# Logits of two heads at a time: three split products on all 128 rows in place of fp32 products on 64 rows

## The chip, the cores and the metric

One NeuronCore of one Trainium2 chip runs the kernel; the other cores are idle. The metric is the device time of one execution in microseconds (us). The engines are named as in the profile: PE is TensorE (its weight loads stand as PEld), DVE is VectorE, ACT is ScalarE, POOL is GpSimd and SP is SyncE, which issues most DMAs here.

## The reference, cut to what matters

The network is a diffusion-transformer block of two layers (differential attention, pooling mixer, each with an FFN), followed by a second block with three attention branches over the same 256 tokens of width 1024, all in float32. The change lies in the second block alone. There the logits of every branch are

```python
# branch A: index scores, exact top-k of the keys, 8 query heads on one key head
rel = jax.nn.relu(jnp.einsum("bqhd,bsd->bqhs", iqb, ik))           # 4 index heads
logits = jnp.einsum("bqhd,bqkd->bhqk", qb, kg) * scale + bias
# branch B: 8 query heads on 2 key heads; compressed, selected and window keys
lc = jnp.einsum("bqghd,bngd->bghqn", qb, kcmp) * scale             # 16 compressed keys
ls = jnp.einsum("bqghd,bgqkd->bghqk", qb, kg) * scale + bias_s
lw = jnp.einsum("bqghd,bkgd->bghqk", qb, kwb) * scale + bias_w
# branch C: 12 heads in three dilated groups under one softmax
```

with heads of 64 features. Each is followed by a masked softmax and the weighted sum of the values; the branches' outputs go through projections and gates and are added.

## The kernel before, in words

All tokens stand as two tiles of 128 (`t` = 0, 1). Features that are contracted lie on the partitions, which are the rows of PE. Large products are made of three: operands are split into a high part of type float32r and the rest (`wsplit`, L57: ACT writes `hi`, DVE `lo` = raw - `hi`), and `mm3` (L77) issues hi*hi, hi*lo and lo*hi. These are lines 78 to 80 in every view.

The second block (from L863) first normalises and transposes the residual stream into `hT` (`to_hT`, L300, PE transposes at L308). Then for each branch it runs `project` (L913: h times a slice of `w_in_2`, two PSUM banks), the normalisation of heads (`head_rstd`, L929), the transposition of queries and keys (`normed_T`, L951; `normed_dup_T`, L961, which puts the same key head on both halves of the partitions), the attention (`attend`, L973), `split_oT` (L1011), `gates` (L1020) and `branch` (L1032). A transposed pair of heads fills 128 partitions, one head on each half. `transpose_to` (L940) transposes on PE (L944) and copies from PSUM with one ACT instruction (L949) into `qT` (two buffers) or the key tile `kk` (`ktile`, L876, one buffer), both plain float32. In branch A the index queries and keys are copied by DVE (L1076, L1077).

`attend` makes the logits of four heads (three in branch C) for one token tile: for each head one fp32 matmul with 64 rows, 128 query columns as weights and `nk` = 128 (t = 0) or 256 (t = 1) keys as the moving operand (L987). Heads of different halves write to different banks of the two-bank tag `s`. Then DVE adds the bias and takes the minimum (L989), ACT does the exponential (L996, joint L992), PE transposes the weights (L1002), DVE copies them (L1003) and PE multiplies by the values (L1007). The index scores of branch A (L1087) and the compressed keys of branch B (L1198, 16 keys a head) are also fp32 products on 64 rows.

The order on each engine is a planner's: it goes by program order as priority and by its own costs, and takes later products (gates and the next projections) where the next ones in program order are not ready. Each engine then runs its list strictly in order. POOL's queue at the start of the block is: load `small` (masks, L887), zero `pr2` (L892), load the small parameters into it (L893, L895), load the bias tiles `W` (L910). PE transposes `pr2` (L897), and the key gains that `normed_dup_T` uses come from there. The top-k of branch A is a run of DVE instructions (L1098, L1099).

Of the kernel before, what the change touches and what calls it, by code (L numbers as in the profile page):

```python
# [31 lines left out]
def tile_net(ctx: ExitStack, tc: tile.TileContext, I: dict, out: bass.AP):  # L32
# [24 lines left out]
    def wsplit(raw, a, b, slot=None):  # L57
        """hi and lo parts of a weight unit; the slots rotate over those of wp (0, 1) and the extra pools."""
# [43 lines left out]
    def mod_group(layer, g):  # L102
        """acc [128, 1024]: summed over its partitions it is the g-th sixth of the modulation."""
# [29 lines left out]
    # relative-position bias rows, by distance 255 .. -127, masks included, with their sign changed; 23 copies in DRAM  # L133
# [20 lines left out]
    # the background stream of modulation work: a generator advanced between weight units  # L154
# [69 lines left out]
    def behind(*ins):  # L224
        """on their engines, what follows is issued after ins."""
# [5 lines left out]
    class Norm:  # L231
        """normalisation over the features, with the tokens on the partitions, a tile of 128 of them after the other."""
# [6 lines left out]
        def pre(self, t, n, P, grow):  # L239
            """half n of tile t of ALPHA times the residual stream plus grow * P, and its sum."""  # L240
# [5 lines left out]
        def squares(self, t, n, v, bias):  # L246
            """the part of half n in the mean of (v + 32 * bias) squared."""
# [10 lines left out]
        def normalise(self, t):  # L258
            """tile t less its mean, over its standard deviation."""
# [11 lines left out]
        def layer_norm(self, t, rows):  # L271
            """the residual stream is tile t less its mean, over its standard deviation, times rows[0], plus rows[1]."""
# [12 lines left out]
        def rms(self, t):  # L285
            """z = tile t of the residual stream over its root mean square."""
# [6 lines left out]
        def residual(self, t, rows):  # L293
            """the residual stream is the affine of the normalised tile."""
# [5 lines left out]
        def to_hT(self, t, hT, A, B=None):  # L300
            """tile t of hT = split of z * A + B, transposed."""
# [14 lines left out]
        def pair(self, b, t, k, hh, hl, A, B):  # L316
            """two chunks of to_hT, from k on."""
# [10 lines left out]
    def ln_rows(l, w):  # L328
        """gain and bias of a layer norm on all partitions."""
# [6 lines left out]
    class Out:  # L336
        """output projection mov^T @ w, a PSUM bank for a half of the features of a tile of tokens; rows of w two
        chunks a unit, the last units held back so that the tiles end one after the other."""
# [22 lines left out]
        def finish(self, t, n):  # L361
            """the bank of half n of tile t."""
# [4 lines left out]
    class Ffn:  # L367
        """the FFN's input products, of the first FIRST pairs of hidden chunks tile by tile."""
# [89 lines left out]
    with tc.tile_pool(name="at", bufs=1, side="right", reuse_waits="tile") as at:  # L458
# [43 lines left out]
        def mod_quarter(q):  # L502
            """modc's columns of the chunks 2q and 2q + 1: the scales plus 1 and the shifts of x and ctx."""
# [41 lines left out]
        class Chunk:  # L545
            """256 columns of w_qkv (two heads of q, k or v): loaded once, the products by chunks of k."""
# [44 lines left out]
        with behind(seq["mod"]):  # L591
# [19 lines left out]
            # lambda  # L611
# [40 lines left out]
            # the maps lie on different halves of the PE rows: taking turns, their products overlap  # L652
# [21 lines left out]
        def head_out(aTs, vt, g, sm):  # L674
            """the two heads' outputs of both tiles, normalised and transposed into oT[:, 2g:2g + 2, :]."""
# [51 lines left out]
        # output projection  # L727
# [8 lines left out]
    def norm_loop(nm, P, row, tail, between=None):  # L736
        """pre, normalise and tail of both tiles; what the second starts with fits the waits of the first."""
# [23 lines left out]
    # FFN of layer 0  # L761
    with tc.tile_pool(name="hid", bufs=1, side="right", reuse_waits="tile") as hidp:
# [8 lines left out]
        # the mixing table and what the mixing makes of the shift, alike for all tokens, wait in the place of hT  # L771
# [6 lines left out]
        def mix(dst, t, q, lhs, first):  # L778
            """dst [128, 256] += the tokens of tile t mixed by pm[:, t, q]: their window's mean less the token itself."""
# [94 lines left out]
    with tc.tile_pool(name="b2", bufs=1, reuse_waits="tile") as b2:  # L874
        # the branches take turns with these
        def ktile():  # L876
            return b2.tile([128, 6, 256], F32, tag="kk", name="kk", bufs=1)
# [7 lines left out]
        # small parameters  # L885
# [27 lines left out]
        def project(c0, n, *after):  # L913
            """two PSUM banks: h2 @ w_in[:, c0:c0 + n] for the two token tiles."""
# [14 lines left out]
        def head_rstd(views, nh):  # L929
            """1 / rms of each 64-wide head of the given [128, nh, 64] views, as [128, len(views) * nh]."""  # L930
# [9 lines left out]
        def transpose_to(dst, src, n, scale=None):  # L940
            """dst [128, n, 128] = transposes of the n [128, 128] blocks of src."""
# [3 lines left out]
            bv = b[:, :n * 128].rearrange("p (n c) -> p n c", n=n)  # L945
# [134 lines left out]
        for t in range(2):  # L1080
# [7 lines left out]
            for h2 in range(2):  # L1088
                se.activation(rel[:, h2:4:2, :nk], Sb[h2][:, :, :nk], AF.Relu)
# [280 lines left out]
```

## Time and profile before

| | us |
|---|---|
| three runs | 1171.26, 1172.57, 1173.49 |
| median | 1172.57 |
| profiled execution: span from the first to the last instruction | 1172.5 |
| PE busy, share of the span | 1140.1 (97%) |
| DVE busy | 815.7 (70%) |
| ACT busy | 568.1 (48%) |
| POOL busy | 78.7 (7%) |

The page gives no time of the profiled execution besides its span, so the span stands for its own time; it lies 0.07 us under the median. Busy is the union of an engine's instructions. Consecutive matmuls overlap in the pipeline: a matmul's own duration is longer than the distance from its start to the start of the next, and the distance is what it costs when PE has always something to do. One fp32 matmul of the program stands in the trace as two MATMUL records, a float32r matmul as one.

### The profile page before, as it was taken

The numbers are of one execution on the slowest core, as the hardware profiler recorded it, in microseconds if no ns is written. First come the engines' busy times: TensorE is split into PE (matmuls) and PEld (weight loads), VectorE is DVE, ScalarE is ACT, GpSimd is POOL, SyncE is SP. The second block draws the span as 40 slices with busy tenths as digits, with TensorE's granted clock in tenths as the row PEclk, the third lists the DMA queues.
The fourth block names the chain that finished last, engine by engine and source line by source line (L and its number), as shares of the span: only waits on it lengthen the run. The fifth ranks groups of instructions, "written<-read, shape, count | busy, mean of one in ns | idle before, by whom it ended". The sixth has DMA issues, their size and how long they took to land.

```text
span 1172.5 us, 19786 instructions
## 1 busy us (share of the span) xinstructions
PE 1140.1 (97%) x7973; PEld 1031.5 (88%) x7973; DVE 815.7 (70%) x1511; ACT 568.1 (48%) x994; POOL 78.7 (7%) x151
## 2 busy tenths in 40 slices
PE   5999999999999999999999899999999999999998
PEld 3889988889999877999988688987999898999986
DVE  4787887887887877766644897776676575655542
ACT  4653443475444436644452754444345265544430
POOL 0011100100111111000000101000000000000000
PEclk8999999999999999999999999999999999999999
DMA  9947555648988993866665443740456145655630
GB/s 309 319 146 233 159 165 180 212 148 267 324 306 298 368 340 104 268 211 233 234 215 171 135 163 108 205 159 10 136 163 218 57 161 175 216 180 181 199 125 36
DMA packets 147274, 229.69 MB, mean 196 GB/s; under 512 B 5420, under 2 KB 118715, under 8 KB 147182
## 3 DMA queue, kind: packets, MB, share of 16 engines
q1 hardware_dynamic: 131616, 176.10, 46.0%
q0 software_dynamic: 14672, 50.63, 13.0%
q10 hardware_dynamic: 894, 1.69, 0.4%
q8 instruction: 63, 1.03, 0.4%
q14 instruction: 29, 0.24, 0.1%
HBM read 226.36 MB, written 2.04 MB: 195 GB/s over the span
## 4 chain that ended last, share of the span: by engine, by line
PE 85%; DVE 7%; issue 4%; ACT 3%; DMA 1%; POOL 0%; SPq 0%; ACTq 0%; POOLq 0%; DVEq 0%
PE mm L78 23%; PE mm L80 23%; PE mm L79 23%; PE s L987 3%; PE tp L1007 2%; DVE wlo L71 2%; PE s L658 1%; PE tp L1002 1%; PE tp L682 1%; DMA raw<-in_w_mod_dram 1%; PE s L118 1%; PE s L511 1%; PE s L510 1%; ACT whi L70 1%; PE tp L944 1%
## 5 line engine op out<-in xcount | busy, mean ns | idle before, releaser
L71 DVE TENSOR_TENSOR wlo<-raw,whi 128x1024 fp32r<-128x1024 f32 (+1 forms) x328 | 383.8, 1192 | 155.4 <-ACT whi L70 155.0
L70 ACT CAST whi<-raw 128x1024 fp32r<-128x1024 f32 (+1 forms) x328 | 325.7, 1028 | 236.7 <-PE mm L79 96.7
L80 PE MATMUL mm<-hTh,wlo 128*128 128x256 f32 x1056 | 299.5, 284 | 0.0
L78 PE MATMUL mm<-hTh,whi 128*128 128x256 f32 x1056 | 298.9, 283 | 0.0
L79 PE MATMUL mm<-hTl,whi 128*128 128x256 f32 x1056 | 298.3, 282 | 0.0
L79 PEld LDWEIGHTS mm<-hTl,whi 128*128 128x128 f32 x1056 | 199.1, 189 | 1.4 <-issue 1.3
L78 PEld LDWEIGHTS mm<-hTh,whi 128*128 128x128 f32 x1056 | 199.1, 188 | 1.5 <-issue 0.7
L80 PEld LDWEIGHTS mm<-hTh,wlo 128*128 128x128 f32 x1056 | 199.1, 189 | 0.6 <-issue 0.3
L78 PE MATMUL mm<-whi,hTh 128*128 128x256 f32 (+4 forms) x592 | 186.2, 315 | 2.4 <-DVE hTh L324 2.3
L79 PE MATMUL mm<-wlo,hTh 128*128 128x256 f32 (+4 forms) x592 | 184.6, 312 | 2.0 <-DVE wlo L71 2.0
L80 PE MATMUL mm<-whi,hTl 128*128 128x256 f32 (+4 forms) x592 | 184.8, 313 | 0.4 <-DVE hTl L325 0.4
L78 PEld LDWEIGHTS mm<-whi,hTh 128*128 128x128 f32 x592 | 112.4, 190 | 10.2 <-DVE hTh L324 3.0
L79 PEld LDWEIGHTS mm<-wlo,hTh 128*128 128x128 f32 x592 | 112.3, 190 | 6.5 <-DVE wlo L71 2.7
L80 PEld LDWEIGHTS mm<-whi,hTl 128*128 128x128 f32 x592 | 112.3, 190 | 5.7 <-issue 1.0
L112 DVE SCALAR_TENSOR_TENSOR acc<-mraw,csil,acc 128x1024 f32<-128x1024 f32 x80 | 102.0, 1278 | 8.2 <-DMA mraw<-in_w_mod_dram 7.8
L78 PE MATMUL mm<-whi,hid 128*128 128x512 f32 x264 | 104.2, 395 | 0.0
L79 PE MATMUL mm<-wlo,hid 128*128 128x512 f32 x264 | 104.1, 394 | 0.0
L80 PE MATMUL mm<-whi,hid 128*128 128x512 f32 x264 | 103.7, 393 | 0.0
L111 POOL DMA_DIRECT2D mraw<-in_w_mod_dram x80 | 42.6, 533 | 363.7 <-DVE acc L112 291.4
L79 PEld LDWEIGHTS mm<-wlo,hid 128*128 128x128 f32 x264 | 49.5, 188 | 11.6 <-issue 1.0
L80 PEld LDWEIGHTS mm<-whi,hid 128*128 128x128 f32 x264 | 49.5, 188 | 11.5 <-issue 0.7
L78 PEld LDWEIGHTS mm<-whi,hid 128*128 128x128 f32 x264 | 49.5, 188 | 11.4 <-issue 0.7
(318 smaller groups left out, 1501.7 us busy)
## 6 DMA issues: line engine op xcount, KB each, us to landing
raw<-in_ffn_w_in_dram SPq DMA_DIRECT2D x44, 1024.0 KB, 6.3
mraw<-in_w_mod_dram POOLq DMA_DIRECT2D x80, 512.0 KB, 5.2
raw<-in_ffn_w_out_dram SPq DMA_DIRECT2D x22, 1024.0 KB, 5.5
raw<-in_w_ffn_in_dram SPq DMA_DIRECT2D x22, 1024.0 KB, 5.2
raw<-in_w_in_dram SPq DMA_DIRECT2D x16, 1024.0 KB, 5.2
raw<-in_attn_w_qkv_dram SPq DMA_DIRECT2D x12, 1024.0 KB, 7.5
raw<-in_w_ffn_out_dram SPq DMA_DIRECT2D x11, 1024.0 KB, 5.1
raw<-in_w_in_dram SPq DMA_DIRECT2D x14, 768.0 KB, 4.4
```

The source lines that it names most:

```text
L70: se.copy(hv[:, sl], raw[:, sl])
L71: seq["sub"] = ve.tensor_sub(lv[:, sl], raw[:, sl], hv[:, sl].bitcast(F32)).ins
L78: pe.matmul(o, lh, rh, start=first, stop=False, **kw)
L79: pe.matmul(o, lh, rl, start=False, stop=False, **kw)
L80: return pe.matmul(o, ll, rh, start=False, stop=last, **kw).ins
L111: gp.dma_start(raw, wv[:, k, g * 1024:(g + 1) * 1024])
L112: ve.scalar_tensor_tensor(acc, raw, csil[:, k, 0:1], acc, op0=ALU.mult, op1=ALU.add)
L118: pe.matmul(b[:, j:j + 1], acc[:, j * 128:(j + 1) * 128], ones[:, 0:1], start=True, stop=True)
L510: pe.matmul(o, lh4[:, k, :], wh, start=k == 0 and w == 0, stop=False, **kw)
L511: pe.matmul(o, lh2[:, k, :], wl, start=False, stop=k == 7, **kw)
L987: pe.matmul(So[i], q[hs, pr, tk], kT[hs, :nk], start=True, stop=True)
L1007: pe.matmul(po[:, c:c + 64], pT[:, kt, i, :], heads[i][5](kt), start=kt == 0 and (not joint or i == 0), stop=kt == t and (not joint or i = ...
```

## The change

Operands of the logits are kept in float32r as a high and a low part. Queries: `qT` becomes [128, pair, hi/lo, 256] with one buffer instead of two. Keys: one tile `KZ` [128, 6, hi/lo, half, 256] for all branches takes the place of `kk`. In its slice `half` only the 64 partitions of that half hold keys; the others are zeroed once by POOL at the start of the block. One matmul with all 128 rows of a query pair as weights and both slices as moving operand (2 x `nk` columns) then gives the logits of both heads, and three such products (hi*hi, lo*hi, hi*lo) make the result. The same goes for the index scores and, with a tile `kcZ`, for the compressed keys. Each copy from PSUM is now an ACT instruction for `hi` and a DVE instruction for `lo`, twice for keys (once for each half of the partitions). In branch C the heads are taken in pairs, so two softmaxes are under way at a time; the transposed weights `pT` are three buffers of 128 keys instead of two of 256. The scratch that software DMAs get in SBUF is set to 4096 bytes a partition. Comments are dropped throughout. The core of the diff:

```diff
-        def ktile():
-            return b2.tile([128, 6, 256], F32, tag="kk", name="kk", bufs=1)
+        KZ = b2.tile([128, 6, 2, 2, 256], F32R, name="KZ")
+        for half in range(2):
+            gp.memset(KZ[(1 - half) * 64:(2 - half) * 64, :, :, half, :].bitcast(F32), 0.0)
...
-        def transpose_to(dst, src, n, scale=None):
+        def transposed(src, n):
             b = tbank()
             for i in range(n):
                 pe.transpose(b[:, i * 128:(i + 1) * 128], src[:, i * 128:(i + 1) * 128], ident)
-            bv = b[:, :n * 128].rearrange("p (n c) -> p n c", n=n)
-            if scale is None:
-                se.copy(dst, bv)
-            else:
-                se.activation(dst, bv, AF.Copy, scale=scale)
+            return b[:, :n * 128].rearrange("p (n c) -> p n c", n=n)
+        def put(hi, lo, src, scale):
+            se.activation(hi, src, AF.Copy, scale=scale)
+            ve.scalar_tensor_tensor(lo, src, scale, hi.bitcast(F32), op0=ALU.mult, op1=ALU.subtract)
+        def put_k(src, t, d0, scale=1.0):
+            n, tk = src.shape[1], slice(t * 128, (t + 1) * 128)
+            for half in range(2):
+                p = slice(half * 64, (half + 1) * 64)
+                put(KZ[p, d0:d0 + n, 0, half, tk], KZ[p, d0:d0 + n, 1, half, tk], src[p],
+                    scale if isinstance(scale, float) else scale[p])
+        def put_q(dst, src, t, d0, scale=1.0):
+            n, tk = src.shape[1], slice(t * 128, (t + 1) * 128)
+            put(dst[:, d0:d0 + n, 0, tk], dst[:, d0:d0 + n, 1, tk], src, scale)
...
-                transpose_to(dst[:, d0:d0 + nh, t * 128:(t + 1) * 128], tmp, nh, scale)
+                put_k(transposed(tmp, nh), t, d0, scale)
...
+        def pair_scores(t, q, pr, kz, nk):
+            S = sbank().rearrange("p (a b) -> p a b", a=2)[:, :, :nk]
+            tk = slice(t * 128, (t + 1) * 128)
+            for i, (a, b) in enumerate(((0, 0), (1, 0), (0, 1))):
+                pe.matmul(S, q[:, pr, a, tk], KZ[:, kz, b, :, :nk], start=i == 0, stop=i == 2)
+            return S
...
-            Sb = [sbank().rearrange("p (a b) -> p a b", a=2) for _ in range(2)]
-            So = [(Sb[i // 2][:, i % 2, :nk] if joint else Sb[heads[i][2]][:, i // 2, :nk]) for i in range(n)]
-            for i in range(n):
-                q, pr, hf, kT, W, v = heads[i]
-                hs = slice(hf * 64, (hf + 1) * 64)
-                pe.matmul(So[i], q[hs, pr, tk], kT[hs, :nk], start=True, stop=True)
...
-            pT = b2.tile([128, 2, 4, 128], F32, tag="pT", name="pT", bufs=2)
+            pT = [b2.tile([128, 4, 128], F32, tag="pT", name="pT", bufs=3) for _ in range(t + 1)]
...
+        def attend(t, q, g, kz, W, po, v):
+            nk = 128 * (t + 1)
+            lg, mx = soft_tiles()
+            Ss = [pair_scores(t, q, 2 * g + i, kz, nk) for i in range(2)]
+            for i in range(2):
+                logits(nk, Ss[i], [W(2 * i), W(2 * i + 1)], lg, mx, (2 * i, 2 * i + 1))
+            return weigh(t, 4, lg, mx, False, po, [(64 * i, v) for i in range(4)])
...
-            ve.tensor_copy(iqT[:, :, tk], b[:, 0:256].rearrange("p (n c) -> p n c", n=2))
-            ve.tensor_copy(ikT[:, tk], b[:, 256:384])
-        normed_dup_T(PA, 0, 1, kAT, 0, GA)
+            bv = b[:, 0:384].rearrange("p (n c) -> p n c", n=3)
+            put_q(iqT, bv[:, 0:2], t, 0)
+            put_k(bv[:, 2:3], t, 0)
+        normed_dup_T(PA, 0, 1, 1, GA)
...
-        qT = b2.tile([128, 6, 256], F32, tag="qT", name="qT", bufs=2)
+        qT = b2.tile([128, 6, 2, 256], F32R, tag="qT", name="qT", bufs=1)
...
+        kcZ = b2.tile([128, 2, 2, 2, 16], F32R, name="kcZ")
+        gp.memset(kcZ.bitcast(F32), 0.0)
...
+            Sc = sbank()[:, 0:128].rearrange("p (r h n) -> p r h n", r=4, h=2)
+            for pr in range(4):
+                for i, (a, c) in enumerate(((0, 0), (1, 0), (0, 1))):
+                    pe.matmul(Sc[:, pr], qT[:, pr, a, tk], kcZ[:, pr // 2, c], start=i == 0, stop=i == 2)
...
+            for jp in range(2):
+                soft = [soft_tiles() for _ in range(2)]
+                for g in range(3):
+                    S = pair_scores(t, qT, 2 * g + jp, 2 * g + jp, nk)
+                    for i in range(2):
+                        logits(nk, S[:, i:i + 1], [WC[g][:, 2 * jp + i, 256 - nk:256]], *soft[i], (g,))
...
-    nc = _bacc.Bacc("TRN2", target_bir_lowering=False, num_devices=1)
+    nc = _bacc.Bacc("TRN2", target_bir_lowering=False, num_devices=1, dynamic_dma_scratch_size=4096)
```

## Rows read from the trace of the kernel before

**Rows 1.** The page: span, part 1 (busy share by engine), part 4 (the chain).
```profile
span 1172.5 us, 19786 instructions
PE 1140.1 (97%) x7973; PEld 1031.5 (88%) x7973; DVE 815.7 (70%) x1511; ACT 568.1 (48%) x994; POOL 78.7 (7%) x151
PE 85%; DVE 7%; issue 4%; ACT 3%; DMA 1%; POOL 0%; SPq 0%; ACTq 0%; POOLq 0%; DVEq 0%
```
**Rows 2.** Windows of the second block: stretch, length, busy by engine, clock, DMA.
```profile
core 0: us, PE busy (x) PEld busy (x) DVE busy (x) ACT busy (x) POOL busy (x), PEclk, DMA share, GB/s
676.00:696.00 20.00, 19.59 (x133) 16.84 (x132) 19.70 (x79) 11.38 (x17) 0.00 (x0) 1.00 0.48 161
...
782.00:823.00 41.00, 41.00 (x280) 31.84 (x280) 28.77 (x123) 20.52 (x74) 3.59 (x7) 1.00 0.12 34
...
845.00:902.00 57.00, 55.44 (x330) 54.14 (x328) 40.61 (x92) 28.65 (x43) 0.00 (x0) 1.00 0.60 188
...
sum 291.00, PE 287.76 PEld 259.15 DVE 209.93 ACT 136.69 POOL 12.71; mean PE 31.97 PEld 28.79 DVE 23.33 ACT 15.19 POOL 1.41
```
**Rows 3.** Groups by line on PE, 660 to 955 us: the products on 64 rows.
```profile
L987 PE MATMUL s<-kk,qT 64*128 64x128 f32 (+1 forms) x144 | 32.7, 358 | 0.0
...
L1198 PE MATMUL s<-kcT,qT 64*128 64x16 f32 x32 | 3.2, 262 | 0.0
...
L1087 PE MATMUL s<-kk 64*128 64x128 f32 (+1 forms) x16 | 1.9, 350 | 0.0
```
**Rows 4.** Timeline of PE (start, us): 64-row runs between others, the first and last included.
```profile
675.76 0.71 PE L1087 MATMUL s<-kk 64*128 64x128 f32 x8
...
700.50 0.28 PE L78 MATMUL mm<-hTh,whi 128*128 128x256 f32 x1
700.71 0.48 PE L987 MATMUL s<-kk,qT 64*128 64x128 f32 x2
701.13 0.33 PE L1002 MATMUL tp<-idsel,lg 128*128 128x128 f32 x1
701.39 0.48 PE L987 MATMUL s<-kk,qT 64*128 64x128 f32 x2
...
924.81 0.70 PE L987 MATMUL s<-kk,qT 64*128 64x256 f32 x2
925.44 0.39 PE L79 MATMUL mm<-hTl,whi 128*128 128x256 f32 x1
925.66 0.28 PE L80 MATMUL mm<-hTh,wlo 128*128 128x256 f32 x1
```
**Rows 5.** Timeline of PE: float32r products of 512 columns; of 256 after transposes.
```profile
672.10 0.40 PE L79 MATMUL mm<-wlo,hTh 128*128 128x512 f32 x1
672.34 0.39 PE L80 MATMUL mm<-whi,hTl 128*128 128x512 f32 x1
...
709.25 0.36 PE L80 MATMUL mm<-hTh,wlo 128*128 128x256 f32 x1
709.46 0.28 PE L78 MATMUL mm<-hTh,whi 128*128 128x256 f32 x1
709.58 0.28 PE L79 MATMUL mm<-hTl,whi 128*128 128x256 f32 x1
```
**Rows 6.** Groups by line and shape, DVE and ACT, 660 to 955 us: nearest to the copies.
```profile
L957 DVE TENSOR_TENSOR qn<-mm,rs 128x384 f32<-128x384 f32 x8 | 4.1, 552 | 0.1
...
L1046 DVE SCALAR_TENSOR_TENSOR yacc<-gate,mm 128x512 f32<-128x512 f32 x4 | 2.7, 679 | 1.5 <-PE mm L80 1.5
...
L1076 DVE COPY kk<-tp 128x256 f32<-128x256 f32 x2 | 0.8, 411 | 0.0
L1077 DVE COPY kk<-tp 128x128 f32<-128x128 f32 x2 | 0.6, 276 | 0.0
...
L949 ACT ACTIVATE kk<-tp,pc 128x384 f32<-128x384 f32 x4 | 2.2, 583 | 1.1 <-PE tp L944 1.1
```
**Rows 7.** POOL: its zero fills before 660 us (groups by line), its first load after (timeline).
```profile
L105 POOL MEMSET acc<- 128x1024 f32 x10 | 9.6, 957 | 97.7 <-DVE hcTl L543 51.7 <-PE s L118 20.0 <-ACT f L323 18.9
...
663.63 0.54 POOL L887 DMA_DIRECT2D small<-in_k_small_dram  x1 [78.25 <-ACT z L291]
```

More of the change, by code (lines that the diff above doesn't have):

```diff
@@ L1002, in attend, with soft_tiles @@
                     pe.transpose(b[:, i * 128:(i + 1) * 128], lg[:, i, kt * 128:(kt + 1) * 128], ident)
-                ve.tensor_copy(pT[:, kt, :n, :], b[:, :n * 128].rearrange("p (n c) -> p n c", n=n))
-            for i in range(n):
-                c = po_cols[i]
+                ve.tensor_copy(pT[kt][:, :n, :], b[:, :n * 128].rearrange("p (n c) -> p n c", n=n))
+            for i, (c, v) in enumerate(vs):
                 for kt in range(t + 1):
-                    pe.matmul(po[:, c:c + 64], pT[:, kt, i, :], heads[i][5](kt),
+                    pe.matmul(po[:, c:c + 64], pT[kt][:, i, :], v(kt),
                               start=kt == 0 and (not joint or i == 0), stop=kt == t and (not joint or i == n - 1))
             return mx[:, 12:13] if joint else mx[:, 12:12 + n]
+        def soft_tiles():
+            return (b2.tile([128, 4, 256], F32, tag="lg", name="lg", bufs=2),
+                    b2.tile([128, 16], F32, tag="mx", name="mx", bufs=3))
+        def attend(t, q, g, kz, W, po, v):
[5 more added lines that the diff above has]
+            return weigh(t, 4, lg, mx, False, po, [(64 * i, v) for i in range(4)])
         def split_oT(o_t, nb, oTh, oTl, t):
@@ L1063, in tile_net @@
         iwc = b2.tile([128, 2, 4], F32, name="iwc")
-        kA = ktile()
-        iqT, ikT, kAT = kA[:, 0:2, :], kA[:, 2, :], kA[:, 3:4, :]
+        iqT = b2.tile([128, 2, 2, 256], F32R, tag="vv", name="iqT", bufs=1)
         for t in range(2):
@@ L1083, in tile_net @@
             rel = b2.tile([128, 4, 256], F32, tag="lg", name="rel", bufs=2)
-            Sb = [sbank().rearrange("p (a b) -> p a b", a=2) for _ in range(2)]
-            for h in range(4):
-                hs = slice((h % 2) * 64, (h % 2 + 1) * 64)
-                pe.matmul(Sb[h % 2][:, h // 2, :nk], iqT[hs, h // 2, tk], ikT[hs, :nk], start=True, stop=True)
-            for h2 in range(2):
-                se.activation(rel[:, h2:4:2, :nk], Sb[h2][:, :, :nk], AF.Relu)
+            for pr in range(2):
+                se.activation(rel[:, 2 * pr:2 * pr + 2, :nk], pair_scores(t, iqT, pr, 0, nk), AF.Relu)
             sco = b2.tile([128, 512], F32, tag="so", name="sco", bufs=2)[:, 0:256]
@@ L1116, in tile_net @@
                 po = tbank()
-                den = attend(t, [(qT, 2 * hg + i // 2, i % 2, kAT[:, 0, :], Wm[:, i, :nk], lambda kt: vA[:, kt, :])
-                                 for i in range(4)], False, po, [0, 64, 128, 192])
+                den = attend(t, qT, hg, 1, lambda i: Wm[:, i, :nk], po, lambda kt: vA[:, kt, :])
                 rden = b2.tile([128, 4], F32, tag="rden", name="rden", bufs=2)
@@ L1176, in tile_net @@
         pe.transpose(b[:, 0:32], cks[:, 2:4, :].rearrange("p a c -> p (a c)"), ident[:32, :32])
-        kcT = b2.tile([128, 32], F32, name="kcT")
-        se.activation(kcT, b[:, 0:32], AF.Copy, scale=GB)
+        kcZ = b2.tile([128, 2, 2, 2, 16], F32R, name="kcZ")
+        gp.memset(kcZ.bitcast(F32), 0.0)
+        for half in range(2):
+            p = slice(half * 64, (half + 1) * 64)
+            put(kcZ[p, :, 0, half, :], kcZ[p, :, 1, half, :], b[p, 0:32].rearrange("p (g n) -> p g n", g=2), GB[p])
         b = tbank()
@@ L1183, in tile_net @@
         PQ = project(964, 512)
-        qT = b2.tile([128, 6, 256], F32, tag="qT", name="qT", bufs=2)
-        normed_T(PQ, 0, 8, qT, 0, QS)
+        qT = b2.tile([128, 6, 2, 256], F32R, tag="qT", name="qT", bufs=1)
+        to_q = lambda b, t, d0, q=qT: put_q(q, b, t, d0, QS)
+        normed_T(PQ, 0, 8, 0, to_q)
         WB = [wtile(8), wtile(12)]
@@ L1192, in tile_net @@
             co = b2.tile([128, 5, 8], F32, tag="co", name="co", bufs=2)
-            Sc = [sbank()[:, 0:64].rearrange("p (h n) -> p h n", n=16) for _ in range(2)]
-            for h in range(8):
-                hs = slice((h % 2) * 64, (h % 2 + 1) * 64)
-                g = h // 4
-                pe.matmul(Sc[h % 2][:, h // 2, :], qT[hs, h // 2, tk], kcT[hs, g * 16:(g + 1) * 16], start=True, stop=True)
+            Sc = sbank()[:, 0:128].rearrange("p (r h n) -> p r h n", r=4, h=2)
+            for pr in range(4):
+                for i, (a, c) in enumerate(((0, 0), (1, 0), (0, 1))):
+                    pe.matmul(Sc[:, pr], qT[:, pr, a, tk], kcZ[:, pr // 2, c], start=i == 0, stop=i == 2)
             pcb = b2.tile([128, 8, 16], F32, tag="pc", name="pc", bufs=1)
-            for h2 in range(2):
-                ve.tensor_add(pcb[:, h2:8:2, :], Sc[h2], nmask[:, t, None, 0:16].to_broadcast([128, 4, 16]))
+            ve.tensor_add(pcb, Sc.rearrange("p r h n -> p (r h) n"), nmask[:, t, None, 0:16].to_broadcast([128, 8, 16]))
             ve.tensor_reduce(co[:, 0, :], pcb, axis=AX.X, op=ALU.min)
@@ L1219, in tile_net @@
                     po = tbank()
-                    den = attend(t, [(qT, 2 * g + i // 2, i % 2, kBT[:, 2 * br + g, :], WB[g][:, i, 256 - nk:256] if t
-                                      else WB[g][:, i, 128:256], lambda kt, c=2 * br + g: vB[:, kt, c, :])
-                                     for i in range(4)], False, po, [0, 64, 128, 192])
+                    den = attend(t, qT, g, 2 * br + g, lambda i: WB[g][:, i, 256 - nk:256], po,
+                                 lambda kt: vB[:, kt, 2 * br + g, :])
                     cc = co[:, 3 + br, 4 * g:4 * g + 4]
@@ L1240, in tile_net @@
                 if kind < 2:
-                    normed_T(PC, 0, 6, (qT, kC)[kind], 3 * hf, (QS, GC)[kind])
+                    normed_T(PC, 0, 6, 3 * hf, (to_q, to_k)[kind])
                 else:
```

51 lines of the change are left out of this document (24 added, 27 removed).

## The prediction

> **What bounds the kernel now.** I read the page first: PE is busy for 97% of the span, and 85% of the chain that ended last is PE's [rows 1]. Then the windows of the second block, where all edits lie: from 664 to 955 us PE is busy 287.76 of 291 us and runs at full clock, DVE 209.93, ACT 136.69 [rows 2]. So time that leaves PE's list there leaves the kernel, as long as PE finds its operands ready; the planner fills the waits of the attention with gate and projection products. One stretch is tight on two engines: from 676 to 696 us, where branch A makes its top-k, DVE is busy 19.70 of 20 us beside PE's 19.59 [rows 2].
>
> Next I looked at what the 64-row products really cost. Durations of matmuls overlap, so I take distances from start to start in PE's timeline. The groups give 32.7 + 3.2 + 1.9 = 37.8 us of busy time for the 64-row records [rows 3], of which the tail of each run lies under the next instruction: the last run is 0.70 us long but the next starts 0.63 after it [rows 4]. There are 47 such runs in PE's list; the rows show the first and the last [rows 4]. 37.8 - 47 x 0.07 = 34.5 us.
>
> The runs also cost at their edges. The float32r product ahead of a run holds PE for 0.21 us (700.50 to 700.71) and the one behind it 0.22 (925.44 to 925.66) [rows 4], where such a product between its like takes 0.12 (709.46 to 709.58) [rows 5]. That is 0.09 + 0.10 = 0.19 a run, 8.9 us in all. Where a run sits between transposes it isn't less: a single one there lasts 0.26 us (701.13 to 701.39) [rows 4]. **The logits now cost PE 34.5 + 8.9 = 43.4 us.**
>
> **The change, part by part.** *New products.* Pairs of heads: branch A 4 for each token tile and 2 of index scores, B 8, C 6, so 20 with 128 keys and 20 with 256. Each is three float32r products, of 256 or of 512 columns. The same type and shape of matmul takes 0.12 and 0.24 us from start to start (672.10 to 672.34) [rows 5]; that weights and keys now come from other tiles doesn't matter for it. 20 x 3 x 0.24 + 20 x 3 x 0.12 = 14.4 + 7.2 = 21.6. The compressed keys need 2 x 4 x 3 = 24 products of 32 columns; I take the 256-column price, 2.9 us, which is too much rather than too little. Together 24.5 us, in place of 34.5.
>
> *New edges.* With all rows in use a float32r product behind another pays nothing. Behind fp32 transposes it does: 0.21 in place of 0.12 (709.25 to 709.46) [rows 5], while nothing shows a price ahead of transposes. At most every run stands so, 47 x 0.09 = 4.2; at least none does, since a gate product behind the transposes pays it today as well. I take the middle, 2.1. **PE after: 26.6 us, so 16.8 us leave its list.** The bounds of the edges make it 14.7 to 18.9.
>
> *Added copies, DVE.* No row shows a copy into 64 partitions; I price it as one of all partitions with the same columns (half is the lower end), and a `lo` by the DVE row of its width: 512 columns 0.679, 384 0.552, 256 0.411, 128 0.276 [rows 6]. Branch A: index queries 2 x 0.411, index keys 4 x 0.276, key head 4 x 0.276, queries 2 x 0.679, less the copies L1076 and L1077, 2 x 0.687: 3.0 us. Branch B: keys 8 x 0.411, queries 2 x 0.679, compressed keys 2 x 0.276: 5.2. Branch C: queries 4 x 0.552, keys 8 x 0.552: 6.6. In all 14.8 us, so DVE in the block goes from 209.93 to some 225 of the about 274 us that would be left. Over the block this is hidden under PE. Where DVE has no room it isn't: branch A's 3.0 us fall almost whole into or just before the full stretch at 676 to 696, ahead of the queries on which the first logits wait. Bounds 0 (PE fills with more gate products) and 3.0; I take 2.5, since DVE there has 0.3 us to spare. In branch C's projections (845 to 902) DVE is at 40.61 of 57 and gets 6.6 more [rows 2]; its mean leaves room, but `lo` parts of keys queue ahead of the next weights' `lo`. Bounds 0 and 2.2 (the second halves of the keys, 4 x 0.552); I take 0.5.
>
> *Added copies, ACT.* 17 more instructions (8, 5 and 4 in the three branches) of at most 0.583 us [rows 6], 9.9 us at most, with ACT under half busy: nothing, hidden under PE; `hi` then `lo` makes each operand later by one DVE copy, which is in the term above.
>
> *POOL.* The two zero fills of `KZ` go to the head of its queue, ahead of `small`, `pr2` and the `W` loads. A fill of 1024 columns took 0.957 us [rows 7], so 3072 columns take 2.9 and both 5.7. They may start only when the earlier owners of that memory are done, as `small` did at 663.63 [rows 7] after 78 us of waiting. PE's transposition of `pr2` and the masks for the index scores wait behind them. Bounds 0 and 5.7. I take 0: the transposed gains aren't used until branch A's key head, behind two projections' worth of products, and the planner knows of the wait. The small fill for `kcZ` is nothing beside this.
>
> *Buffers and the rest.* With one `qT`, a branch's queries wait for the last logits of the branch before; a whole output projection and two input projections lie between, so nothing. Three `pT` and two softmaxes under way in branch C tie transposes to the value products one attention back: nothing where PE has other products. The smaller DMA scratch changes no instruction of PE; POOL is busy 78.7 us [rows 1], and I cost it at nothing. None of these can come out below nothing, but the planner's new order can go either way by a microsecond or two.
>
> **Sum**, against the profiled span of 1172.5 us, which is 0.1 under the median: 1172.5 - 16.8 + 2.5 + 0.5 = **1158.7 us**.
>
> **Rivals.** *Half of it comes back: the softmax takes over.* In 782 to 823 us, mostly branch B's attention, PE is busy throughout and DVE 28.77 of 41.00 [rows 2]. Branch B holds 16 of the 40 pairs, so PE's list there shrinks by 16/40 of 16.8 = 6.7 to 34.3, and DVE stands at 84% of that, on a chain (logits, exponential, transposes, copy, values) that can't be packed tightly. For it: little else is in PE's list there. Against: the gate products of branch B come right behind and can be drawn in. If half the gain is lost, 1172.5 - 8.4 + 1 = 1165. The Trainium skill, in TensorEngine Tiling (Array Packing), section PSUM Bottleneck, says that once TensorE is made faster the copy out of PSUM can become the limit; no run here shows at which speed-up it would.
>
> *Nothing moves.* The zero fills and branch A's DVE work are both paid in full (5.7 + 3.0), the keys of C too (2.2), and half of what is left of the gain is lost in waits: 1172.5 - (16.8 - 10.9)/2 = 1169.6, or up to 1171 with the upper edge price: within 0.2%.
>
> *Slower: the split is on the path.* Every added copy stands between a transposition and the logits: PE, in strict order, waits for ACT's `hi`, then DVE's `lo`, because one buffer each of `qT` and `KZ` leaves no lead. Then 14.8 + 9.9 = 24.7 us are exposed against 16.8, 1172.5 + 7.9 = 1180.4. It decides where over 68% of the added copies is exposed. Against: PE waited for a total of 291 - 287.76 = 3.2 us in the whole block [rows 2], with the same kind of copies in place.
>
> *More than forecast.* No edge prices, no loss: 1172.5 - 18.9 = 1153.6; a shorter path could give another 1 or 2.
>
> That the products would run at fp32's rate isn't among them: their tiles are float32r, like those in [rows 5].
>
> **How the numbers follow.** Forecast (1154 to 1163) 0.66; half comes back (1163 to 1168) 0.15; more (under 1154) 0.06; nothing moves 0.07; slower 0.06. The range for 8 in 10 is 1153 to 1167: it holds the forecast, most of the half and of the better end. A measurement of this kernel can tell 0.2%, 2.3 us, from no change. Faster than that: 0.66 + 0.15 + 0.06 and a small part of the fourth case, 0.88; within it 0.06; slower 0.06.
>
> **What would show it.** Right: no 64-row records on PE; 120 float32r products for the logits, 0.24 and 0.12 us apart; gate products next to them at 0.12, not 0.21; PE still busy over 97% from 664 us to the end of branch C, which comes some 14 us earlier; time before 664 us and after the block unchanged. Wrong: PE idle ahead of L897 or of the index scores (POOL's fills), ahead of branch A's first logits (DVE), or PE waiting for `pT` and `lg` in the attention. The forecast fails if those idle times sum to more than 10 us, or if the new products stand further apart than rows of their shape do.

## The result, and the profile of the changed kernel

The changed kernel takes **1163.64 us** (median of 4 runs, 1160.9 to 1164.32), the kernel before 1173.03 on the same chip: a ratio of **0.9914** (95% interval 0.9893 to 0.9935), so 10.1 us faster by the ratio (the medians differ by 9.4). A second set of runs gave 0.9914 again. Some executions of the kernel before and of its variants ran 1.5% and more longer at a lower granted clock; they count in the medians given here, not in the ratios. The prediction was 1158.7 with 1153 to 1167 as its range: right in direction and inside the range, 3.7 us short of the forecast gain of 13.8. The measured time lies 0.6 us above the band of 1154 to 1163 that the prediction gave to its own mechanism.

The profiled run took 1160.9 us, its span 1159.1. The page of the changed kernel, beside [rows 1]:

```profile
span 1159.1 us, 19748 instructions
PE 1125.4 (97%) x7925; PEld 1030.3 (89%) x7925; DVE 829.4 (72%) x1541; ACT 574.7 (50%) x1011; POOL 84.0 (7%) x154
```

PE lost 14.7 us of busy time; DVE gained 13.7 (the `lo` copies, priced at 14.8 net; the 36 of them last 17.5 in all), ACT 6.6, POOL 5.3. The span fell by less than PE's busy time. Where the rest went is read in the windows, beside [rows 2] (stretch, length, busy by engine, clock, DMA):

```profile
684.00:692.00 8.00, 6.22 (x40) 6.26 (x41) 7.96 (x27) 4.27 (x9) 0.00 (x0) 0.79 0.00 0
...
782.00:823.00 41.00, 40.90 (x320) 37.99 (x319) 33.89 (x130) 22.71 (x77) 4.19 (x8) 1.00 0.20 58
...
845.00:902.00 57.00, 55.69 (x347) 54.35 (x346) 48.33 (x128) 31.72 (x50) 0.00 (x0) 1.00 0.62 202
```

Branch B's attention (782 to 823) and branch C's projections (845 to 902) are as full on PE as before, with DVE 5 and 8 us busier under it: those copies are hidden. (The changed kernel runs ahead, so the same clock times hold somewhat later work; the runs without copies, below, bear it out.) The one disturbed stretch is 684 to 692, where PE is idle for nearly 2 us and its mean granted clock is 0.79. PE's timeline there (start, duration, what; in brackets the idle time before it and what ended it):

```profile
677.10 0.30 PE L900 MATMUL tp<-idsel,pr 128*128 128x128 f32 x1 [0.49 <-DMA pr<-in_qk_norm_g_dram]
...
683.52 0.40 PE L80 MATMUL mm<-whi,hTl 128*128 128x512 f32 x1
685.77 0.30 PE L947 MATMUL tp<-idsel,kn 128*128 128x128 f32 x1 [1.85 <-DVE kn L986]
...
686.55 0.42 PE L79 MATMUL mm<-hTl,whi 128*128 128x256 f32 x1
686.77 0.41 PE L80 MATMUL mm<-hTh,wlo 128*128 128x256 f32 x1
...
689.76 0.33 PE L79 MATMUL mm<-hTl,whi 128*128 128x256 f32 x1
...
690.28 0.28 PE L80 MATMUL mm<-hTh,wlo 128*128 128x256 f32 x1
690.40 0.28 PE L78 MATMUL mm<-hTh,whi 128*128 128x256 f32 x1
```

Three things are to be seen. `pr2`'s transposition waits 0.49 us for its load. The key head's transposition waits 1.85 us for DVE; before, it had no wait. Then the gate products stand some 0.21 us apart (686.55 to 686.77), at TensorE's lower level of 1.2 GHz, until 689.76, and 0.12 apart after it. The 15 products from 686.55 to 689.76 lose about 15 x 0.095 = 1.4 us. POOL's timeline shows why the load is late:

```profile
665.00 5.38 POOL L880 MEMSET KZ<- 64x3072 f32 x2 [81.74 <-DVE hTl L325]
670.34 0.54 POOL L890 DMA_DIRECT2D small<-in_k_small_dram  x1
...
671.89 1.06 POOL L898 DMA_DIRECT2D pr<-in_qk_norm_g_dram  x2
```

The fills take 5.38 us (5.7 forecast) at the head of the queue, and they may start only behind DVE's `hTl`, 1.4 us later than `small` did before. `small` itself leaves at 670.34, where before it left at 663.63 [rows 7]: 6.7 us later by the clock, and 8.8 counted from the start of the block, which comes 2.1 us earlier in this profile.

The new products are what the prediction said. Groups by line on PE, 664 to 930 us, of the changed kernel in its second set of runs:

```profile
L994 PE MATMUL s<-KZ,qT 128*128 128x512 f32 x54 | 17.6, 426 | 0.0
L994 PE MATMUL s<-KZ,qT 128*128 128x256 f32 x54 | 10.6, 304 | 0.2 <-DVE mx L1000 0.2
L1226 PE MATMUL s<-kcZ,qT 128*128 128x32 f32 x24 | 3.0, 258 | 0.1
```

With the 12 for the index scores these are the 120 float32r products and the 24 for the compressed keys; no product on 64 rows is left. Start to start they and their own edges hold PE for 26.6 us, which is the forecast.

**A ledger of the block.** Below, "the block" runs from the last transposition of the normalised tile ahead of it (L308, 663.77 us before) to the last one of the next such tile (986.02 before). That is 322.2 us before, 311.0 in the profile above and 311.4 in the second one. It leaves out the first block, which the change doesn't touch and whose end lies anywhere from 661.5 to 667.5 us in the profiles of all kernels; what follows takes 186.4 or 186.5 us in each. Profiles of the same kernel agree within 0.4 us on the block, so it tells kernels apart better than the times do. I split it by summing PE's distances from start to start, with what exceeds 0.6 us counted as waits.

### The profile page after: what moved, and what is told of

Same layout as the page of the kernel before. It is cut to its first block, busy times and chain, and to the rows that moved or that the text cites. A ratio compares the mean times of both kernels' runs of the same rounds, so it can differ in the third digit from the quotient of the medians.

```text
span 1159.1 us, 19748 instructions
## 1 busy us (share of the span) xinstructions
PE 1125.4 (97%) x7925; PEld 1030.3 (89%) x7925; DVE 829.4 (72%) x1541; ACT 574.7 (50%) x1011; POOL 84.0 (7%) x154
## 5 line engine op out<-in xcount | busy, mean ns | idle before, releaser
L71 DVE TENSOR_TENSOR wlo<-raw,whi 128x1024 fp32r<-128x1024 f32 (+1 forms) x328 | 384.5, 1193 | 140.0 <-ACT whi L70 139.6
L112 DVE SCALAR_TENSOR_TENSOR acc<-mraw,csil,acc 128x1024 f32<-128x1024 f32 x80 | 102.1, 1280 | 10.8 <-DMA mraw<-in_w_mod_dram 10.3
```

Source lines behind the costliest of these rows:

```text
L71: seq["sub"] = ve.tensor_sub(lv[:, sl], raw[:, sl], hv[:, sl].bitcast(F32)).ins
L112: ve.scalar_tensor_tensor(acc, raw, csil[:, k, 0:1], acc, op0=ALU.mult, op1=ALU.add)
```

## The experiments

Kernels that ran together were held against the kernel before on the same chip (medians 1174.2, 1174.1 and 1175.7 us). Edits start from the changed kernel where nothing else is said.

**The changed kernel again**, as the anchor.

> The changed kernel as it is, for reference in this set. Its gain over the kernel before: 8 to 12 us (ratio 0.990 to 0.993). PE should stand idle or at half clock for some 4 us between 675 and 693 us.

1163.29 us, ratio 0.9914 (0.9893 to 0.9934). Its profile has the same wait of 1.85 us for the key head, and the same 3.4 us at 1.2 GHz behind it.

**The fills behind the small loads.** If the fills cost by standing ahead of `pr2` on POOL's queue, they should cost nothing behind it.

```diff
-        KZ = b2.tile([128, 6, 2, 2, 256], F32R, name="KZ")
-        for half in range(2):
-            gp.memset(KZ[(1 - half) * 64:(2 - half) * 64, :, :, half, :].bitcast(F32), 0.0)
         small = b2.tile([128, 554], F32, name="small")
...
-            gp.dma_start(pr2[32:38, dup * 64:(dup + 1) * 64], I["qk_norm_g_2"][0])
+            last_small = gp.dma_start(pr2[32:38, dup * 64:(dup + 1) * 64], I["qk_norm_g_2"][0])
...
         pos = pc2[:, 0:32].rearrange("p (s l) -> p s l", s=2)
+        KZ = b2.tile([128, 6, 2, 2, 256], F32R, name="KZ")
+        with behind(last_small.ins):
+            for half in range(2):
+                gp.memset(KZ[(1 - half) * 64:(2 - half) * 64, :, :, half, :].bitcast(F32), 0.0)
```

> The zero fills of KZ are issued by POOL behind the loads of small and pr2 instead of ahead of them; nothing else is edited. Theory POOL (the fill delays pr2, and with it the index scores and top-k of branch A): PE's transposition of pr2 comes some 5 us earlier, the first logits of branch A 5 to 7 us earlier, and the kernel is 3 to 5 us faster than the changed one. Rival DVE (the added lo copies delay branch A): the same time as the changed kernel within 1 us.

1159.64 us, ratio 0.9884 (0.9868 to 0.990): 3.65 us faster than the changed kernel. POOL's timeline and the window from 676 us of this kernel:

```profile
663.75 0.54 POOL L887 DMA_DIRECT2D small<-in_k_small_dram  x1 [78.29 <-ACT z L291]
...
665.31 1.05 POOL L895 DMA_DIRECT2D pr<-in_qk_norm_g_dram  x2
666.40 5.42 POOL L906 MEMSET KZ<- 64x3072 f32 x2
671.76 2.16 POOL L914 DMA_DIRECT2D W<-scr  x4
```

```profile
676.00:696.00 20.00, 19.82 (x126) 17.30 (x126) 19.39 (x69) 13.27 (x23) 0.00 (x0) 1.00 0.70 215
```

The same fills take the same 5.42 us and now cost nothing that shows: no wait for the key head, full clock. The block falls from 311.4 to 307.8 us, 3.6 less: 1.65 of waits (2.90 to 1.25) and 2.0 in the gate and projection products (233.96 to 231.99), the same products at full clock. The late fills do touch DVE: the cast of `hTh` that begins 0.1 us behind the first of them lasts 2.71 us, as long as one fill, where the two just ahead of it take 0.28 and 0.29, while the weight splits under the early fills keep their 1.2 us. PE, busy with products whose operands are there, doesn't wait for that cast.

**The fills twice**, each one issued two times in its old place, to see whether the loss grows with their length.

```diff
-        for half in range(2):
+        for half in (0, 1, 0, 1):
             gp.memset(KZ[(1 - half) * 64:(2 - half) * 64, :, :, half, :].bitcast(F32), 0.0)
```

> Each zero fill of KZ is issued twice, so POOL's first load of the block is another 5.4 us later. Theory POOL: branch A's first logits come about 5 us later, the kernel is 2 to 5 us slower than the changed one. Rival DVE: the same within 1 us.

1169.67 us, ratio 0.9966 (0.9953 to 0.9979): 6.4 us slower than the changed kernel, for 5.4 us more on POOL, and more than the 2 to 5 us of the theory. The windows and the waits of PE:

```profile
684.00:692.00 8.00, 3.15 (x13) 2.27 (x13) 5.15 (x17) 3.37 (x11) 0.66 (x2) 0.74 0.47 124
692.00:700.00 8.00, 6.51 (x23) 5.43 (x24) 7.19 (x31) 3.89 (x9) 0.00 (x0) 0.50 0.28 108
```

```profile
PE tp L900 <- DMA pr<-in_qk_norm_g_dram: 3.3, 1, 3.3
PE s L994 <- ACT KZ L952: 1.9, 2, 1.1
```

Now PE waits 3.3 us for the load alone, then four more times, and the stretch from 692 us has a mean clock of 0.50. The waits of the block grow by 4.7 us and the block by 5.9 (311.4 to 317.3): a longer stall costs more than its own length.

**No `lo` copies.** The copies are left out, and the products that read `lo` read `hi`. So hi times hi is added three times and the logits are three times too large (not rounded, as the expectation has it); the number and the shapes of PE's products are the same. DVE loses 36 instructions, not 42.

```diff
             se.activation(hi, src, AF.Copy, scale=scale)
-            ve.scalar_tensor_tensor(lo, src, scale, hi.bitcast(F32), op0=ALU.mult, op1=ALU.subtract)
...
-            for i, (a, b) in enumerate(((0, 0), (1, 0), (0, 1))):
+            for i, (a, b) in enumerate(((0, 0), (0, 0), (0, 0))):
...
```

> The lo copies on DVE are left out, and all three products read the hi parts, so the logits are rounded: PE's list is the same, DVE loses 42 instructions, 14.8 us by the prediction's rows. Theory POOL: at most 1 to 2 us faster than the changed kernel, because DVE is hidden but for the stretch of the top-k. Rival DVE: 3 to 5 us faster, the whole difference between the time forecast and the one measured.

1159.97 us, ratio 0.9884 (0.9869 to 0.9899): 3.3 us faster than the changed kernel, more than the theory of the fills allowed. Read alone, this says that DVE's 3.0 us of the prediction were right. The last set of runs puts it otherwise.

**One product of three.** The two with a `lo` part are left out, so the logits lack the low part; fills and copies stay.

```diff
-            for i, (a, b) in enumerate(((0, 0), (1, 0), (0, 1))):
-                pe.matmul(S, q[:, pr, a, tk], KZ[:, kz, b, :, :nk], start=i == 0, stop=i == 2)
+            for i, (a, b) in enumerate(((0, 0),)):
+                pe.matmul(S, q[:, pr, a, tk], KZ[:, kz, b, :, :nk], start=i == 0, stop=i == 0)
...
```

> The changed kernel with one of the three split products of each logit pair (hi times hi), the two others left out; the copies and the fills stay. In the changed kernel the logit products take 26.6 us of PE's list, so two thirds of it, about 17 us, go. If PE's list sets the end of the second block, the time falls by 15 to 18 us against the changed kernel: ratio to before 0.976 to 0.979. The rival is that VectorE's softmax work has become the limit in this block: then less than half comes back, 8 us or less, ratio 0.984 or more, and PE shows as many more microseconds of waits on DVE in the block.

1156.67 us, ratio 0.9857 (0.9844 to 0.9871): 6.7 us less, where PE's list lost 17.1 us of logits (26.6 to 9.5, start to start). The rival's number, but not yet its place; the waits of PE, 655 to 930 us:

```profile
PE tp L947 <- DVE kn L986: 5.3, 1, 5.3
PE tp L308 <- ACT z L291: 2.5, 1, 2.5
PE tp L1043 <- DVE oB L1255: 1.9, 1, 1.9
```

The longest is the key head's, the wait that the fills make. So the edit had to be tried again without them (below).

**The smaller scratch alone**, in the kernel before.

```diff
-    nc = _bacc.Bacc("TRN2", target_bir_lowering=False, num_devices=1)
+    nc = _bacc.Bacc("TRN2", target_bir_lowering=False, num_devices=1, dynamic_dma_scratch_size=4096)
```

> The kernel before with nothing but the smaller scratch for the descriptors of POOL's DMAs (4096), which is the part of the change that was priced at 0. Both theories: ratio 0.998 to 1.002. If it is not, the scratch carries some of what was put down to the fills. It is also what the next kernel is to be held against.

1174.16 us, ratio 1.0002 (0.9992 to 1.0012): nothing, as priced.

**The fills in the kernel before**, with the smaller scratch, into a buffer that nobody reads.

```diff
+        KZ = b2.tile([128, 3072], F32, name="KZ")
+        for half in range(2):
+            gp.memset(KZ[(1 - half) * 64:(2 - half) * 64], 0.0)
...
         small = b2.tile([128, 554], F32, name="small")
```

> The kernel before with the smaller scratch and two fills of 64x3072 zeros on POOL (2.66 us each, 5.3 in all) ahead of the small loads, into a buffer that nobody reads; nothing else of the change. If the fills cost by delaying the loads behind them on POOL's queue, the loss is here too: 2.5 to 5 us slower than before (moving the fills behind the loads gained 3.65), ratio 1.002 to 1.0045, and the transposition of the small load waits for its DMA. The rival is that the loss needs the changed kernel itself (the first logits wait for the filled buffer, or the wait is hidden where the old products fill PE): 1 us at most, ratio under 1.001.

1174.92 us, ratio 1.0008 (0.9996 to 1.002): 0.9 us slower, where the theory asked for at least 2.5. The rival's number, by another way than it said, as PE's timeline shows:

```profile
680.45 0.30 PE L901 MATMUL tp<-idsel,pr 128*128 128x128 f32 x1 [0.91 <-DMA pr<-in_qk_norm_g_dram]
...
687.86 0.33 PE L948 MATMUL tp<-idsel,kn 128*128 128x128 f32 x1 [0.95 <-DVE kn L974]
...
688.73 0.28 PE L80 MATMUL mm<-hTh,wlo 128*128 128x256 f32 x1
688.85 0.28 PE L78 MATMUL mm<-hTh,whi 128*128 128x256 f32 x1
```

The fills do delay the load, and PE does wait, 0.91 and 0.95 us; but the second wait is half as long as in the changed kernel, and the products behind it stand 0.12 us apart: no half clock. The block is 323.8 us, 1.5 more than before. In the kernel before, the fills are worth 1 to 1.5 us, not 3.6.

**fp32 on all rows**, from the kernel with late fills: one fp32 product over both heads with the padded keys, no split, no `lo` copies.

```diff
-        KZ = b2.tile([128, 6, 2, 2, 256], F32R, name="KZ")
+        KZ = b2.tile([128, 6, 1, 2, 256], F32, name="KZ")
...
-            for i, (a, b) in enumerate(((0, 0), (1, 0), (0, 1))):
+            for i, (a, b) in enumerate(((0, 0),)):
```

> The changed kernel with the fills behind the small loads, but the logits as one fp32 product over both heads on 128 rows with the padded keys, no split and no lo copies. It tells apart what the rows and what the number format are worth. If the 64-row form is the costly thing (its slow products and the switch of rows), one fp32 product of 512 columns takes four float32r passes of 0.234 us, 0.94 us, against 0.70 for three split products: logits of about 32 us on PE's list against 24.5 and edges of 2.1 in the changed kernel; with VectorE's lo copies gone (3.3 us) the time is 0 to 4 us above that of the changed kernel with late fills, ratio 0.989 to 0.992. The rival is that fp32 is the costly thing: a pair of heads takes twice the 0.63 us of one head of 256 keys, the list falls by little more than the edges, and the time is 8 to 12 us above it, ratio 0.995 to 0.999.

1161.25 us, ratio 0.9907 (0.9891 to 0.9923): 2.7 us above late fills, inside the first theory's range. One pair in PE's timeline:

```profile
712.25 0.84 PE L1018 MATMUL tp<-idsel,lg 128*128 128x128 f32 x4
712.93 1.02 PE L994 MATMUL s<-KZ,qT 128*128 128x512 f32 x2
713.79 0.60 PE L1018 MATMUL tp<-idsel,lg 128*128 128x128 f32 x4
```

The pair takes 713.79 - 712.93 = 0.86 us as two records, against 0.94 expected and 0.70 for three float32r products. So of the gain of the version with late fills (about 13.6 us), some 10.9 are had with plain fp32 on all rows, and some 2.7 by the three split products.

**Three on one chip**: late fills again; late fills without `lo` copies (the logits three times too large, as above); late fills with one product of three (the other two left out). Their edits are those above, put together.

> The changed kernel with the fills behind the small loads, once more, as what the next two are held against on the same chip: ratio 0.987 to 0.990 to before in every theory.

> The changed kernel with the fills behind the small loads and without the lo copies on VectorE (their products read the hi parts, so the logits lack the low part). Without the late fills the copies were worth 3.3 us. If they cost that by VectorE's time through the whole block, both gains add up: 2.5 to 4 us faster than with late fills alone, ratio 0.985 to 0.986. If the copies cost mostly through the stall at the start of the block, where the fills made PE wait and its clock fell, the late fills have taken that already: 1.2 us at most, ratio 0.987 or more, and no stretch at half clock in 676 to 696 us in either kernel.

> The changed kernel with the fills behind the small loads and one of the three split products of each logit pair. With the early fills this took 17.6 us of logits off PE's list and gave back 6.7 us. If the rest was lost to the stall that the fills make at the start (PE's wait for the keys of 5.3 us and the half clock after it), most of it returns here: 12 to 16 us faster than late fills alone, ratio 0.975 to 0.978. If VectorE and ScalarE limit the block as soon as PE's list is shorter, the gain stays at 5 to 9 us, ratio 0.981 to 0.984, with PE's waits on DVE and ACT in several places and half clock behind them.

Late fills: 1160.04 us, 0.9879 (0.9858 to 0.990). Without `lo`: 1162.16 us, 0.9896 (0.9877 to 0.9916), block 307.7 us against 308.2. With the fills late the copies cost nothing that shows, and the 2.5 us by which they were to add up are not there. The four cases side by side, ratio to before, length of the block in the profiled run, and PE's waits in it:

| | with `lo` copies | without |
|---|---|---|
| fills early | 0.9914; 311.0 and 311.4 us; 2.9 us | 0.9884; 308.6 us; 3.8 us |
| fills late | 0.9884 and 0.9879; 307.8 and 308.2 us; 1.3 us | 0.9896; 307.7 us; 1.4 us |

By time only the case with both is slow, but the step from it to early fills without copies, 0.0030, has an interval of some 0.0025 either way. The profiles don't bear out that the copies make the loss. **The early fills cost PE 1.6 us of waits with the copies and 2.4 without.** What the case with both has more is time at the lower clock, 3.4 us behind the key head's wait, in both of its profiles. The profile of early fills without copies has full clock throughout the block, in spite of its waits, and even in its first stretch, where the kernels don't differ yet. The first window of the kernel before, and then two of early fills without copies:

```profile
664.00:676.00 12.00, 11.46 (x52) 9.79 (x53) 10.72 (x22) 8.87 (x21) 4.33 (x9) 0.86 0.71 198
...
664.00:676.00 12.00, 11.57 (x54) 9.65 (x54) 9.55 (x16) 9.14 (x21) 8.25 (x9) 1.00 0.45 143
...
676.00:696.00 20.00, 17.30 (x115) 14.86 (x114) 16.05 (x64) 12.71 (x25) 1.64 (x4) 1.00 0.54 164
```

3.4 us at half clock cost a busy PE about 1.7 us, so 1.7 of the 2.8 us between the two blocks with early fills can't be put down to the copies. Whether the copies bring about the other stretch at half clock isn't shown.

One product of three with late fills: 1155.71 us, 0.9846 (0.9814 to 0.9877), 3.9 us less by the ratios and 4.5 by the block: less than either theory asked for. So the stall at the start was not what ate the gain of the early one. Waits of PE, 655 to 990 us, and three windows:

```profile
PE tp L308 <- ACT z L291: 3.5, 2, 2.5
PE tp L1044 <- DVE oB L1256: 2.2, 1, 2.2
...
PE mm L78 <- ACT oTh L1047: 1.3, 2, 0.7
PE tp L1023 <- DVE pT L1020: 1.2, 3, 0.5
```

```profile
736.00:744.00 8.00, 6.81 (x41) 6.13 (x41) 5.19 (x21) 0.58 (x1) 0.00 (x0) 0.79 0.73 256
...
820.00:828.00 8.00, 5.09 (x40) 4.25 (x39) 7.26 (x13) 2.21 (x4) 1.55 (x3) 1.00 0.55 161
828.00:832.00 4.00, 3.46 (x15) 3.17 (x15) 1.64 (x3) 0.42 (x1) 0.00 (x0) 0.57 0.99 316
```

The waits now lie at the ends of the attention of branches A and B: `pT`, `oA`, `oB`, `oTh`. DVE is busy 7.26 of 8 us in the stretch that holds the longest one, and half clock follows behind it. What DVE does ahead of `oB`:

```profile
824.28 1.22 DVE L71 TENSOR_TENSOR wlo<-raw,whi 128x1024 fp32r<-128x1024 f32 x1
825.41 0.42 DVE L1254 TENSOR_TENSOR ot<-tp,co 128x256 f32<-128x256 f32 x1
825.75 1.22 DVE L71 TENSOR_TENSOR wlo<-raw,whi 128x1024 fp32r<-128x1024 f32 x1
826.88 0.42 DVE L1256 TENSOR_TENSOR oB<-oB,ot 128x256 f32<-128x256 f32 x1
```

Splits of the next weights (L71) stand in its list between the instructions that PE waits for. In the ledger, 16.6 us leave the logits (26.8 to 10.1), and 2.9 of waits, 3.4 of slower gate and projection products and 5.8 in the other transposes and products come back.

## Why the prediction was right, and which terms were not

**PE's list.** Right in kind, 2.4 us too large. The block of the version with late fills, whose waits are those of before, is 14.4 us shorter (322.2 to 307.8), against 16.8. The new side came out (26.6). The old side didn't: the products of the logits hold PE 33.8 us, not 34.5, and the edges were taken at 0.19 a run everywhere. The step that failed is "Where a run sits between transposes it isn't less". The row that it rests on shows a single transposition between two runs holding 0.26 us [rows 4]; two of them hold 0.37 (kernel before):

```profile
716.85 0.44 PE L1002 MATMUL tp<-idsel,lg 128*128 128x128 f32 x2
717.22 0.70 PE L987 MATMUL s<-kk,qT 64*128 64x256 f32 x2
```

So the second one, with its like ahead of it, takes 0.11, and the single one carries 0.15 for the end of one run and the start of the next, not 0.19. Summed over the neighbours of all 47 runs, each against the median of its like, the edges were 7.7 us, not 8.9; with the 0.7 above that is 1.9 of the 2.4. The prediction also misread the clock: from 664 us PE did not run "at full clock", since its first window, shown above, has 0.86; the sum doesn't use it.

**DVE in branch A, 2.5, and in branch C, 0.5.** Not there: with late fills the block is as long with the copies as without. In branch C they lie under PE, as the windows show. With the fills early the times without the copies are 3.3 us shorter, but the profiles give PE no less waiting there, so a price of the copies in branch A isn't shown.

**POOL, 0.** This is the term that failed: "I take 0: the transposed gains aren't used until branch A's key head, behind two projections' worth of products". The gains weren't what was late. PE takes its instructions in order, `pr2`'s transposition stands ahead of the index transposes, and DVE's copies of these, with the new `lo` parts, ahead of the norm of the key head. The load came 8.8 us later in the block, DVE had its copies and the norm to do in a shorter stretch, and PE ran dry for 1.85 us, with half clock behind. DVE begins the norm 17.7 us after the block's start before, 23.6 in the changed kernel and 20.8 with late fills, where PE doesn't wait for it. The bound of 5.7 held, and the wrong-signals named the first of the two places ("PE idle ahead of L897 or of the index scores": 0.49 us), not the longer one.

So the sum by the runs is -14.4 + 0 + 3.6 = -10.8 for the block of the changed kernel, where the prediction had -16.8 + 3.0 + 0 = -13.8. Two terms were too large in opposite directions and nearly cancelled (2.4 and 3.0), which is luck; the unpriced one makes the difference.

**Rivals.** *Half of it comes back by the softmax* has the nearest number (1165), but its place shows no loss: 782 to 823 us has PE busy 40.90 of 41. It is what happens one step further: of the next 16 us of logits taken off PE's list only some 4 leave the time. The Trainium skill, in TensorEngine Tiling (Array Packing), section PSUM Bottleneck, says that the copy out of PSUM may limit once TensorE is faster. The trace doesn't show that for the changed kernel, nor plainly for the one with one product: its longest new wait is for DVE's `oB`, ahead of which stand 0.42 us of reading PSUM (`ot`) and 2.44 of splitting weights. *Nothing moves* named fills and DVE work as the thieves, which was right of the fills, at too high a price. *Slower* and *more than forecast* have nothing for them.

**What beats both**: the changed kernel with its fills behind the small loads, 0.9884 and 0.9879 of before, 3.65 us faster than the changed kernel on the same chip. (One product of three is faster still, with less exact logits.)

## What to carry to other kernels

A fill or load at the head of a queue is priced by everything queued behind it and by who, on an engine that takes its work in order, waits for the first of those; "not used until later" is checked against the order of that engine. Runs that differ in two edits are compared by their profiles' waits and clock too: here one of four cases had full clock where the others hadn't, and by its time alone the loss would be put down to the copies. And what a second cut of the same list is worth must be measured again: here the first 14 us were worth all of themselves, the next 16 a quarter.

## What was not expected of the hardware

- **The rows were worth more than the number format.** fp32 on all rows, half of its keys zeros, keeps 10.9 us of the gain (0.9907). A head that stood alone in the kernel before held PE for 0.63 us at 256 keys [rows 4], so two cost 1.26, against 0.86 for the pair on all rows. The Trainium skill, in TensorEngine Tiling (Array Packing), section Key Properties, says that a change of tiling mode drains TensorE; the trace is in line with it, as the edges of the runs show (7.7 us for 47). But the 10.9 us are not all a price of changing: two heads on different halves that follow each other ran at the same time in the kernel before.

```profile
707.31 0.70 PE L987 MATMUL s<-kk,qT 64*128 64x256 f32 x4
707.95 0.38 PE L79 MATMUL mm<-hTl,whi 128*128 128x256 f32 x1
```

These four records are two heads; they start within 0.01 us of each other and hold PE for 0.64 us together, less than the 0.70 of three split products. Only about a quarter of the heads at L987 stood so in PE's list. Issuing the old products in such pairs is a rival to this change that no run tried.
- **A stall is followed by half clock, not always.** Behind the wait of 1.85 us the granted clock fell to 1.2 GHz for 3.4 us; in the kernel with fills twice, behind waits of 3.3, 1.1, 0.8, 1.1 and 1.1 us in a row, it stood there for 13.7 us. Behind waits of 0.91 and 0.95 it stayed at 2.4 GHz, and so it did in the profile of early fills without copies, which waited 2.3 us for the same load. The wait of 2.55 us for `z` at the start of the block, where the kernels don't differ yet, has 3.4 us of half clock behind it in 11 of the 13 profiles and none in two. So the same wait can go either way; what decides is left open.
- **Starts of records aren't all prices.** A float32r product behind an fp32 transposition holds PE 0.20 us in place of 0.12, which the prediction counted as an edge (2.1 us in all). In the changed kernel the transposition ahead of it holds 0.02 in place of 0.11:

```profile
710.10 0.27 PE L1018 MATMUL tp<-idsel,lg 128*128 128x128 f32 x1
710.12 0.36 PE L994 MATMUL s<-KZ,qT 128*128 128x256 f32 x1
710.32 0.28 PE L79 MATMUL mm<-hTl,whi 128*128 128x256 f32 x1
```

Together they take 0.22, the sum of the two alone: the record only begins early. How the 14.4 us divide between logits and their neighbours is blurred by this; their total is not.
